# A bidirectional Gated DeltaNet layer on one core: chains emitted by a nominal clock, another way to the 4-block operand, low parts moved to VectorE, fewer row factors

## The chip, the cores and the metric

One core of a Trainium2 chip. TensorE (PE), VectorE (DVE), ScalarE (ACT), GpSimd (POOL) and SyncE (SP, which issues most DMA) each work through their own instruction stream in order. The metric is device microseconds of the whole program; the kernel before took 1396.1 us (median of three runs, 1393.63 to 1396.11).

## The reference

An encoder of two layers over 512 positions and 1024 channels, float32. Layer 0 mixes tokens by a bidirectional gated DeltaNet, layer 1 by a bidirectional gated linear attention (GLA); each is followed by a squared-ReLU MLP, and after each of the four sublayers comes a layer norm of `alpha * x + sublayer(x)`. The change lies in the DeltaNet layer, and in a helper for inverse square roots that all norms use. Of the DeltaNet, cut to what matters (8 heads, 128 channels each, both directions):

```python
qkv = silu(depthwise_conv(proj[..., :3072], conv_w))     # 5 taps
q, k = l2norm(q) * 128 ** -0.5, l2norm(k)
gc = cumsum(g)                                           # in a chunk
decay_mat = exp(where(causal, gc[:, None] - gc[None, :], -inf))
a_mat = where(strict, (k * beta) @ k.T * decay_mat, 0)
sol = triangular_solve(a_mat + I, [v * beta, k * beta * exp(gc)])
# scan over chunks:
v_new = u_c - w_c @ state
o = qd_c @ state + qk_c @ v_new
state = state * gl_c + kd_c.T @ v_new
# both directions added:
o = rmsnorm(o, norm_g) * silu(z);  out = o @ w_out
```

## The kernel before

The kernel takes chunks of 128 rows, so a head has 4 chunks (NT) in each of two directions, 8 units (U). Activations lie with channels on the partitions. Products that need more than one float pass are made in three (`mm3`, L109 to L111): the operands are split into a rounded high part and the rest (`split`, L90 on ScalarE and L91 on VectorE), and high x high, high x low and low x high are added. Weights come by DMA from SP in blocks of 512 KB, three buffers deep.

Per head there are these generators of class `GdnHead`:

- `project`: four projections of 24 matmuls each, tiles pjk, pjq, pjv, pjz; the convolution on ScalarE (L1077) and VectorE (L1081, four taps).
- `rows`: transposes of k and q (ktp), squares with row sums on ScalarE, then small row operations: the logarithms of the row factors, three bfloat16 parts of a row (rsp), their transposes (rtp), and the factors neg and kds.
- `solve`: kk = k k^T; the exponentials E of the decays for both directions (ep, L1208); at = E x kk without its diagonal (L1210); its float16 high part ath (a cast on ScalarE, L1212) and low part atl (a subtraction on GpSimd, L1213); a4, the 4 x 4 diagonal blocks of ath (L1216, all 8 units in one operation). From a4 come the inverses of the 4-blocks in three groups of products hp; then Dd, its transpose Xd (xp), and the inverse of the whole chunk by doubling over block sizes 4, 8, 16, 32 and 64 (products lv, L1265; L1274, L1284, L1285 on VectorE), one correction step with ath and atl (nw), and xf, the inverse as float32 (L1330).
- `recur`: four steps with three products each per direction (tiles m: m1 with the state, L1357; m2 with xf, L1365; m3 with k, L1377), with r on VectorE (L1359), vd and vn on ScalarE and the next state sn; then op, the head's output (L1390).
- `finish`: the RMS norm of op on ScalarE and VectorE (`rsqrt`, L167 to L173), the product fo, its transposes otp (L1413), the gate (L1415), and a split into oh and ol.

`out_pieces` (tile oa) multiplies heads 0 to 5 with w_out; `out_last` (tile ob) does heads 6 and 7 with the layer norm of each of the four row tiles behind it. The masks of the GLA layer (`sel_masks`, L504) are made on GpSimd, in the buffer of tag fo.

The order of the instructions is made in two stages. The program emits the generators in some order, and a scheduler then orders each engine's stream from that, by dependencies, free buffers and a priority that falls with the place in the emission. Before, `gdn` emits whole generators: in round i `recur` of head i-2, `solve` of head i-1, `project` and `rows` of head i, then `finish` of head i-2. The pairs of numbers that the generators yield are not read.

## Time and profile before

| what | value |
|---|---|
| median of three runs | 1396.1 us |
| profiled execution | 1403.4 us, span 1401.7 us |
| TensorE busy | 1361.3 us, 7917 matmul records |
| VectorE, ScalarE, GpSimd busy | 931.5, 693.9, 160.3 us |
| DeltaNet, its heads' stage | about 40 to 426 us of the span |
| of these 386 us | PE busy 377.1, DVE 296.8, ACT 246.6, POOL 37.4 |
| end of the DeltaNet, begin of the MLP | about 426 to 500 us, PE busy 63.1 of 74 |

A row of instructions names line, engine, operation, the tile written and the tiles read. A PE row's busy time runs to the modelled end of a pipelined matmul, so that consecutive ones overlap; start to start is the pace. A float32 product that isn't rounded stands as two records. The heads' stage has the only section in which many short chains over all engines run beside the large products.

### The profile page before, as it was taken

To read this page: it belongs to the slowest core of one execution; us is meant where nothing else is said; L and a number is where in the kernel's file an instruction comes from. 1 tells how busy PE (TensorE), PEld (TensorE's weight loads), DVE (VectorE), ACT (ScalarE), POOL (GpSimd) and SP (SyncE) were. 2 spreads that over 40 slices of the span, in tenths; PEclk is the share of its full clock that TensorE was granted. 3 is DMA by queue.
4 is the path that set the end of the run, shared out by engine and by line. 5 is a ranking of instruction groups with operands and counts; after the bars stand their busy time and mean duration, and the time that the engine had idled before them with its cause. 6 is when DMAs were issued, how large, how long until landed. Compare 5 with 4: busy or idle time off the path is not lost.

```text
span 1401.7 us, 20184 instructions
## 1 busy us (share of the span) xinstructions
PE 1361.3 (97%) x7917; PEld 1119.6 (80%) x7917; DVE 931.5 (66%) x1534; ACT 693.9 (50%) x1318; POOL 160.3 (11%) x228
## 2 busy tenths in 40 slices
PE   7999999999998989999999999999999999999997
PEld 6777777777776878888888888888879788888886
DVE  5787787778767355555655767977865555656655
ACT  3666657665733444444453255654433544545430
POOL 6000400000001301121000100000003111111000
PEclk9999999999999999999999999999999999999999
DMA  6312111111231955574513132212227776656121
GB/s 171 76 46 61 46 46 46 48 47 44 63 118 47 280 132 173 135 180 117 125 60 102 55 116 62 71 50 76 75 61 210 186 186 153 155 130 133 50 80 56
DMA packets 148055, 142.63 MB, mean 102 GB/s; under 512 B 9503, under 2 KB 124311, under 8 KB 147959
## 3 DMA queue, kind: packets, MB, share of 16 engines
q1 hardware_dynamic: 132224, 86.72, 21.7%
q0 software_dynamic: 15168, 54.54, 16.1%
q8 instruction: 62, 1.02, 0.3%
q14 instruction: 34, 0.28, 0.1%
q10 hardware_dynamic: 567, 0.08, 0.0%
HBM read 114.05 MB, written 2.10 MB: 83 GB/s over the span
## 4 chain that ended last, share of the span: by engine, by line
PE 80%; ACT 7%; DMA 4%; issue 4%; DVE 3%; POOL 1%; SPq 0%; DVEq 0%; POOLq 0%; ACTq 0%
PE pj L109 7%; PE pj L111 7%; PE pj L110 7%; PE pjv L109 3%; PE pjv L110 3%; PE pjv L111 3%; PE pX L110 2%; PE pX L109 2%; PE pX L111 2%; DMA w2r<-in_mlp_w 2%; PE pl L109 2%; PE pl L111 2%; PE pl L110 2%; PE scp L729 2%; PE op L1390 2%
## 5 line engine op out<-in xcount | busy, mean ns | idle before, releaser
L91 DVE TENSOR_TENSOR wl<-wst,wh 128x1024 fp32r<-128x1024 f32 x137 | 168.8, 1233 | 206.1 <-ACT wh L90 205.7
L90 ACT CAST wh<-wst 128x1024 fp32r<-128x1024 f32 x137 | 143.9, 1050 | 267.5 <-PE pj L110 168.7
L109 PE MATMUL pj<-xth,wh 128*128 128x512 f32 (+1 forms) x544 | 203.7, 375 | 8.0 <-ACT h L298 7.3
L111 PE MATMUL pj<-xth,wl 128*128 128x512 f32 (+1 forms) x544 | 202.8, 373 | 0.0
L110 PE MATMUL pj<-xtl,wh 128*128 128x512 f32 (+1 forms) x544 | 202.7, 373 | 0.0
L91 DVE TENSOR_TENSOR w2l<-w2r,w2h 128x1024 fp32r<-128x1024 f32 x84 | 102.6, 1222 | 80.6 <-ACT w2h L90 80.5
L109 PEld LDWEIGHTS pj<-xth,wh 128*128 128x128 f32 x544 | 103.1, 190 | 27.2 <-ACT h L298 8.5
L111 PEld LDWEIGHTS pj<-xth,wl 128*128 128x128 f32 x544 | 103.1, 190 | 18.2
L110 PEld LDWEIGHTS pj<-xtl,wh 128*128 128x128 f32 x544 | 103.2, 190 | 17.8
L90 ACT CAST w2h<-w2r 128x1024 fp32r<-128x1024 f32 x84 | 88.2, 1050 | 57.1 <-DMA w2r<-in_mlp_w 24.9
L329 POOL DMA_DIRECT2D w2r<-w2r x48 | 41.9, 912 | 274.0 <-DVE w2l L91 161.3
L90 ACT CAST ah<-h 128x1024 fp32r<-128x1024 f32 x40 | 42.2, 1054 | 41.6 <-PE pX L110 16.8
L110 PE MATMUL pX<-w2l,ah 128*128 128x512 f32 x144 | 56.1, 390 | 0.0
L109 PE MATMUL pX<-w2h,ah 128*128 128x512 f32 x144 | 56.1, 390 | 0.0
L111 PE MATMUL pX<-w2h,al 128*128 128x512 f32 x144 | 56.1, 390 | 0.0
L109 PE MATMUL pjv<-wh,xth 128*128 128x512 f32 x128 | 54.7, 428 | 0.0
L91 DVE TENSOR_TENSOR al<-h,ah 128x1024 fp32r<-128x1024 f32 x40 | 48.9, 1223 | 7.3 <-ACT ah L90 5.7
L1213 POOL TENSOR_TENSOR atl<-on,ath 128x512 f16<-128x512 f32 x16 | 20.9, 1308 | 282.5 <-PE m L1377 149.2
L168 ACT ACTIVATE rsy<-rsv 128x1 f32<-128x1 f32 (+1 forms) x28 | 5.7, 204 | 95.1 <-DVE rsv L167 95.0
L111 PE MATMUL pjv<-wh,xtl 128*128 128x512 f32 x128 | 50.2, 392 | 0.0
L110 PE MATMUL pjv<-wl,xth 128*128 128x512 f32 x128 | 49.9, 390 | 0.0
L312 POOL DMA_DIRECT2D w2r<-in_mlp_w x48 | 36.0, 768 | 115.5 <-DVE w2l L91 94.3
(436 smaller groups left out, 3483.1 us busy)
## 6 DMA issues: line engine op xcount, KB each, us to landing
wst<-in_mlp_w SPq DMA_DIRECT2D x80, 512.0 KB, 4.2
w2r<-in_mlp_w POOLq DMA_DIRECT2D x48, 512.0 KB, 4.6
w2r<-w2r POOLq DMA_DIRECT2D x48, 512.0 KB, 5.7
wst<-in_a_w_in SPq DMA_DIRECT2D x32, 512.0 KB, 4.0
wst<-in_b_w_in SPq DMA_DIRECT2D x32, 256.0 KB, 3.1
wst<-in_a_w_out SPq DMA_DIRECT2D x8, 512.0 KB, 3.8
wst<-in_b_w_in SPq DMA_DIRECT2D x8, 512.0 KB, 3.9
wst<-in_b_w_out SPq DMA_DIRECT2D x8, 512.0 KB, 3.6
```

The lines of the kernel that those rows point to most:

```text
L90: nc.scalar.copy(hi, src)
L91: nc.vector.tensor_tensor(lo, src, hi.bitcast(F32), ALU.subtract)
L109: mm(ps, ah, bh, start=start, stop=False, **kw)
L110: mm(ps, ah, bl, start=False, stop=False, **kw)
L111: mm(ps, al, bh, start=False, stop=stop, **kw)
L168: nc.scalar.activation(y, v, AF.Ln)
L312: nc.gpsimd.dma_start(t, w2[r:r + 2 * P, 512 * j:512 * j + 512].rearrange("(k p) n -> p k n", p=P))
L329: nc.gpsimd.dma_start(blocks[a + (q,)], blocks[b + (q,)], accum_op=ALU.add)
L729: T.matmul(ps[:, n, :], kh[:, sl], qh[:, sl], start=True, stop=True)
L1213: G.tensor_tensor(atl[:, us, :], at, ath[:, us, :], ALU.subtract)
L1390: T.matmul(op[:, n, :], l, r, start=i == 0, stop=i == len(mm) - 1)
```

## The change

1. **Emission.** `gdn` no longer emits whole generators. Six chains per head (project, rows, solve, recur, attend, finish), and the masks and the two halves of the output product, get a nominal start (40 units from head to head) and a factor. The one that is due first is advanced by one yield; its due time grows by the factor times the two numbers yielded. A yielded name waits until that step is done. The products op become a chain of their own, `attend`; `finish` of a head waits for a4 of the next, and `solve` of a head for `finish` two heads back.
2. **The 4-block operand.** kk is multiplied by a second mask (nd4: 4-blocks without the diagonal) into kk4, in the buffer fo; a4 is E x kk4, one operation per direction, written as float16. at and the cast to ath come behind it. The gate product p moves from the buffer on to fo.
3. **Low parts.** atl is subtracted on VectorE, emitted inside the solver's levels 8 and 16, and not on GpSimd.
4. **Row factors.** neg is no longer negated (signs go into qd, the states and sn), kds is one exponential without the product with beta, the factors -0.5 and the small constants go into existing operations, the RMS norm takes its epsilon as a tensor instead of multiplying by fq three times, and `rsqrt` has one operation less.

```diff
@@ rsqrt
-        nc.vector.tensor_scalar(v, x, scale, eps, ALU.mult, ALU.add)
-        nc.scalar.activation(y, v, AF.Ln)
+        if isinstance(eps, float):
+            nc.vector.tensor_scalar(v, x, -0.5 * scale, -0.5 * eps, ALU.mult, ALU.add)
+        else:
+            nc.vector.scalar_tensor_tensor(v, x, -0.5 * scale, eps, ALU.mult, ALU.subtract)
+        nc.scalar.activation(y, v, AF.Ln, scale=-2.0)
         nc.scalar.activation(y, y, AF.Exp, scale=-0.5)
         nc.vector.tensor_tensor(t, y, y, ALU.mult)
         nc.vector.tensor_tensor(t, t, v, ALU.mult)
-        nc.vector.tensor_scalar(t, t, -0.5, 1.5, ALU.mult, ALU.add)
-        nc.vector.tensor_tensor(out, y, t, ALU.mult)
+        nc.vector.scalar_tensor_tensor(out, t, 1.5, y, ALU.add, ALU.mult)
@@ gdn
-            if old:
-                run(old.recur(done))
-            if mid:
-                run(mid.solve(done))
-            if new:
-                run(new.project(done), new.rows(done))
...
-            if old:
-                run(old.finish(done))
+        T = 40
+        todo = []
+        for h, head in enumerate(heads):
+            todo.append([(h - 1) * T + 5, 1.8, head.project(done)])
+            todo.append([(h - 1) * T + 30, 1, head.rows(done)])
+            todo.append([h * T, 1, head.solve(done)])
+            todo.append([(h + 1) * T + 0, 1.5, head.recur(done)])
+            todo.append([(h + 1) * T + 30, 1.5, head.attend(done)])
+            todo.append([(h + 1) * T + 35, 1, head.finish(done)])
+        todo.append([2.5 * T, 1.0, masks()])
+        for hf in range(2):
+            todo.append([(A_H - 1 + hf) * T + 5, 1.8, output(hf)])
+        now = 0.0
+        while todo:
+            todo.sort(key=lambda x: x[0])
...
+            else:
+                todo[k][0] = t + scale * (step[0] + step[1])
@@ rows
-        V.tensor_scalar(lnr, ssp, 1e-6, None, ALU.add)
-        A.activation(lnr, lnr, AF.Ln)
-        V.tensor_scalar(lnr[:, 0, :], lnr[:, 0, :], -0.5, None, ALU.mult)
-        V.tensor_scalar(lnr[:, 1, :], lnr[:, 1, :], -0.5, -0.5 * math.log(P), ALU.mult, ALU.add)
+        A.activation(lnr, ssp, AF.Ln, bias=g.eps[:, 0:1])
...
-        A.activation(neg, rw, AF.Exp)
-        V.tensor_scalar(neg, neg, -1.0, None, ALU.mult)
-        V.tensor_tensor(kds, c0, g.tot[:, :, :, h], ALU.add)
-        A.activation(kds, kds, AF.Exp)
-        V.tensor_tensor(kds, kds, g.beta[:, :, :, h], ALU.mult)
+        A.activation(self.ew, rw, AF.Exp)
+        V.tensor_tensor(self.kds, cj, g.tot[:, :, :, h], ALU.add)
+        A.activation(self.kds, self.kds, AF.Exp)
@@ solve
+        kk4 = self.t2("fo", 1)
+        V.tensor_tensor(kk4, kk, g.nd4.unsqueeze(1).to_broadcast([P, NT, P]), ALU.mult)
+        kks = self.t2("on", 2)
+        V.tensor_tensor(kks, kk, g.nd.unsqueeze(1).to_broadcast([P, NT, P]), ALU.mult)
...
-            at = kks if d else self.t2("on", 2)
-            V.tensor_tensor(at, e, kks, ALU.mult)
-            us = slice(d * NT, (d + 1) * NT)
-            A.copy(ath[:, us, :], at)
-            G.tensor_tensor(atl[:, us, :], at, ath[:, us, :], ALU.subtract)
+            V.tensor_tensor(a4[:, dirs[d], :], e, kk4, ALU.mult)
             ex.append(e)
-        a4 = t8("a4", 1)
-        V.tensor_tensor(a4, ath, g.same4.unsqueeze(1).to_broadcast([P, U, P]), ALU.mult)
+        for d, e in enumerate(ex):
+            V.tensor_tensor(at[d], e, kks, ALU.mult)
+            A.copy(ath[:, dirs[d], :], at[d])
...
+            if s in (8, 16):
+                us = dirs[s // 16]
+                V.tensor_tensor(atl[:, us, :], at[s // 16], ath[:, us, :], ALU.subtract)
@@ finish
+        yield "op", self.h
+        if self.h < A_H - 1:
+            yield "a4", self.h + 1
...
-        V.tensor_tensor(ss, ss, self.fq, ALU.mult)
-        V.tensor_tensor(ss, ss, self.fq, ALU.mult)
-        c.rsqrt(rs_, ss, NT, 1.0 / P, RMS_EPS)
-        V.tensor_tensor(rs_, rs_, self.fq, ALU.mult)
+        c.rsqrt(rs_, ss, NT, 1.0 / P, self.heps)
```

Matmuls are the same in number (8843) in both programs. VectorE has 1478 instructions instead of 1536, GpSimd 218 instead of 233. SP's stream is the same.

Where instructions stand now. VectorE, head 4, from the kk products to the 4-block operand; first before (r and sn belong to the recurrence of head 3, sil to a convolution, on is at):

```order
L1359 SCALAR_TENSOR_TENSOR r<-m_3048,neg,vt 128x128
L1359 SCALAR_TENSOR_TENSOR r<-m_3052,neg,vt 128x128
L1195 TENSOR_TENSOR qd<-sil,qd 128x512
L1210 TENSOR_TENSOR on<-E,on 128x512
L1382 SCALAR_TENSOR_TENSOR sn<-sn,egl,m_3068 128x128
L1382 SCALAR_TENSOR_TENSOR sn<-sn,egl,m_3072 128x128
L1359 SCALAR_TENSOR_TENSOR r<-m_3076,neg,vt 128x128
L1359 SCALAR_TENSOR_TENSOR r<-m_3080,neg,vt 128x128
L1210 TENSOR_TENSOR on<-E,on 128x512
L1382 SCALAR_TENSOR_TENSOR sn<-sn,egl,m_3096 128x128
L1382 SCALAR_TENSOR_TENSOR sn<-sn,egl,m_3100 128x128
L1216 TENSOR_TENSOR a_3173<-ath,same_387 128x1024
```

and with the change:

```order
L1219 TENSOR_TENSOR on<-kk,nd 128x512
L1414 SCALAR_TENSOR_TENSOR sn<-sn,egl,m_3117 128x128
L1414 SCALAR_TENSOR_TENSOR sn<-sn,egl,m_3121 128x128
L1228 SCALAR_TENSOR_TENSOR qd<-sil,qd 128x512 x2
L1391 SCALAR_TENSOR_TENSOR r<-m_3138,neg,vt 128x128
L1391 SCALAR_TENSOR_TENSOR r<-m_3142,neg,vt 128x128
L1111 SCALAR_TENSOR_TENSOR sil<-pjq,cw,sil 128x511
L1242 TENSOR_TENSOR a_3156<-E,fo 128x512
L1111 SCALAR_TENSOR_TENSOR sil<-pjq,cw,sil 128x511
L1242 TENSOR_TENSOR a_3156<-E,fo 128x512
L1111 SCALAR_TENSOR_TENSOR sil<-pjq,cw,sil 128x510
L1245 TENSOR_TENSOR on<-E,on 128x512
```

The masked product fo<-kk (L1217) stands just ahead of the rows shown. The operand a comes from E in two halves, ahead of the products into on. VectorE again, head 4, from the inverse of the 4-blocks (Dd) into the solver's first level, before and with the change:

```order
L1231 TENSOR_TENSOR Dd<-dc,same_387 128x1024
L1081 SCALAR_TENSOR_TENSOR sil<-pjv,cw,sil 128x510
L91 TENSOR_TENSOR wl<-wst,wh 128x1024
L1274 TENSOR_TENSOR pz_174<-lv,off_397 128x2x64x4
L1081 SCALAR_TENSOR_TENSOR sil<-pjv,cw,sil 128x511
L1284 TENSOR_TENSOR Dd<-Dd,lv 128x2x64x4
```

```order
L1262 TENSOR_TENSOR Dd<-dc,same_389 128x1024
L1111 SCALAR_TENSOR_TENSOR sil<-pjv,cw,sil 128x510
L1317 TENSOR_TENSOR atl<-on,ath 128x512
L1303 TENSOR_TENSOR pz_174<-lv,off_400 128x2x64x4
L1317 TENSOR_TENSOR atl<-on,ath 128x512
L1313 TENSOR_TENSOR Dd<-Dd,lv 128x2x64x4
```

Both low parts stand around the first pz, earlier than the emission has them. TensorE at the stage's end, from the output op of head 7 (L1390 before, L1429 now) to its transposes otp; before, op and one L109 stand just ahead of the first row:

```order
L110 MATMUL ob<-wl,oh_423 128x512
L111 MATMUL ob<-wh,ol 128x512
L250 MATMUL ob<-z,ident 128x512
L109 MATMUL ob<-wh,oh_423 128x512
L110 MATMUL ob<-wl,oh_423 128x512
L111 MATMUL ob<-wh,ol 128x512
L250 MATMUL ob<-z,ident 128x512
L109 MATMUL ob<-wh,oh_423 128x512
L110 MATMUL ob<-wl,oh_423 128x512
L111 MATMUL ob<-wh,ol 128x512
L250 MATMUL ob<-z,ident 128x512
L1413 MATMUL otp<-ident,fo 128x128 x4
```

and with the change:

```order
L1429 MATMUL op<-sn,qd 128x128
L252 MATMUL ob<-z,ident 128x512
L109 MATMUL ob<-wh,oh_426 128x512
L110 MATMUL ob<-wl,oh_426 128x512
L111 MATMUL ob<-wh,ol 128x512
L252 MATMUL ob<-z,ident 128x512
L109 MATMUL ob<-wh,oh_426 128x512
L110 MATMUL ob<-wl,oh_426 128x512
L111 MATMUL ob<-wh,ol 128x512
L252 MATMUL ob<-z,ident 128x512
L1452 MATMUL otp<-ident,fo 128x128 x4
```

Nine products with weights and three with the identity stood between op and otp; now six and three do.

95 lines of the change are left out of this document (61 added, 34 removed).

## The prediction

> **What bounds the kernel now.** I read the first part of the page, then busy time by windows, then TensorE's waits in the DeltaNet stage. The page gives the profiled execution's span and the engines:
>
> ```profile
> span 1401.7 us, 20184 instructions
> PE 1361.3 (97%) x7917; PEld 1119.6 (80%) x7917; DVE 931.5 (66%) x1534; ACT 693.9 (50%) x1318; POOL 160.3 (11%) x228
> ```
>
> TensorE looks full, but its busy time counts the modelled tail of every matmul. The count of matmuls per window tells more. The windows below are the heads' stage of the DeltaNet, two steady heads in it, the next two, and 100 us of the MLP; PE's entry comes first, then weight loads, VectorE, ScalarE, GpSimd.
>
> ```profile
> 40.00:426.00 386.00, 377.14 (x3135) 296.32 (x3134) 296.83 (x642) 246.58 (x678) 37.40 (x55) 1.00 0.21 58
> 164.30:256.60 92.30, 89.46 (x762) 70.32 (x760) 73.44 (x159) 60.63 (x169) 4.66 (x4) 1.00 0.18 47
> 256.60:348.60 92.00, 89.17 (x762) 70.27 (x760) 73.40 (x159) 60.58 (x169) 4.67 (x4) 1.00 0.17 47
> 500.00:600.00 100.00, 100.00 (x438) 82.30 (x437) 61.24 (x61) 48.09 (x56) 13.72 (x17) 1.00 0.55 139
> ```
>
> In the MLP a 512-column matmul comes every 100/438 = 0.228 us and nothing else limits. A DeltaNet head takes 46.1 us for 381 matmul records. The pitch of short ones is in the chain of waits (the group's time over its count):
>
> ```profile
> 383.39 3.14 PE op L1390 x28
> 389.71 0.25 PE lv L1265 x8
> ```
>
> That is 0.112 us for 128-column float records and 0.031 us for the solver's. A head has 96 projection matmuls (21.9 us), 84 float records of 128 columns (9.4), 120 solver products (3.7) and 81 others, between 0.031 and 0.112 each (2.5 to 9.1): 37.5 to 44.1 us. So 2.0 to 8.6 us of each head is TensorE standing still inside its in-order stream, and VectorE, at 73.4 of 92.3 us, is busy but not the bound. TensorE's longest waits between 40 and 426 us (engine and line, waited for, us in total, times, longest):
>
> ```profile
> PE hp L1224 <- DVE a L1216: 2.2, 3, 0.9
> PE pjz L109 <- DVE sil L1081: 1.0, 3, 0.3
> PE m L1365 <- DVE r L1359: 0.9, 2, 0.5
> PE ktp L1127 <- ACT junk L1132: 0.9, 4, 0.2
> ```
>
> These are single links, and short. The number of matmuls does not change, so the change can only move such waits, in 8 heads, and shorten what TensorE waits for at the stage's end.
>
> **The change, part by part.** *The 4-block operand.* One of the three hp waits, head 4, in order of time:
>
> ```profile
> 240.95 0.65 ACT L1212 CAST ath<-on 128x512 f16<-128x512 f32 x1
> 241.68 1.16 POOL L1213 TENSOR_TENSOR atl<-on,ath 128x512 f16<-128x512 f32 x1 [1.88 <-ACT ath L1212]
> 241.95 1.44 DVE L1216 TENSOR_TENSOR a<-ath,same 128x1024 f16<-128x1024 f16 x1
> 243.44 0.35 PE L1224 MATMUL hp<-icc,a 128*128 128x4 f16 x8 [0.62 <-DVE a L1216]
> ```
>
> L1216 must follow the casts of both directions, and it slows down beside GpSimd's subtraction. All of its executions, L1210's and L1213's (ns minimum/median/maximum):
>
> ```profile
> L1216 DVE TENSOR_TENSOR a<-ath,same x8: 677/1342/1652, 72.1 to 378.6; 128x1024 f16<-128x1024 f16 x8
> L1210 DVE TENSOR_TENSOR on<-E,on x16: 679/705/1468, 68.1 to 376.4; 128x512 f32<-128x512 f32 x16
> L1213 POOL TENSOR_TENSOR atl<-on,ath x16: 1159/1166/2102, 69.7 to 378.7; 128x512 f16<-128x512 f32 x16
> L1202 DVE TENSOR_TENSOR on<-kk,nd x8: 679/688/692, 64.6 to 370.4; 128x512 f32<-128x512 f32 x8
> ```
>
> Now the operand is two products of 0.68 us (L1210's minimum, same size) straight from the exponentials, each releasing half of the hp group, and the casts come later. Between the last exponential and hp, a product, a cast of 0.65 and 0.7 to 1.65 us of L1216 become one product: about 1.5 us, against a longest wait of 0.9. What is late next are the exponentials:
>
> ```profile
> L1208 ACT ACTIVATE E<-ep,cj 128x128 f32<-128x128 f32 x64 | 19.5, 397 | 0.0
> ```
>
> Eight take 3.2 us, with a product and the steps between 4.4; the new order has hp's second half 5.7 us of TensorE work behind the first ep in heads 4 to 6, hp's first half 4.5 (four exponentials and a product, 2.6). Both fit, if ScalarE is free within a microsecond. I remove the 2.2 us; bounds 0 and -2.6 (three times 0.9).
>
> VectorE pays, per head, 0.69 for the second masked product of kk (L1202), two products of 0.68, and two low parts; before it ran L1216. The low part on VectorE is not in the trace. L1216 did twice the columns in 0.68, and L1210 the same columns in 0.68, so it costs 0.34 to 0.68; I take 0.68. That is 3.4 us added against 1.2 removed, and about nine row operations of 0.16 us (1.5) go. The net +0.7 us lies in a queue that is idle 9 us of each head, and counts nothing by itself; without that cover it would be 5.6 us over 8 heads.
>
> The page "SBUF — State Buffer" of the Trainium skill (section "SBUF: two separate sides") says that VectorE with two inputs in SBUF and GpSimd reading SBUF share an exclusive port pair: whoever comes second is held until the other has finished. The trace agrees: L1216 began 0.27 us into L1213's 1.16, and took 1.44 instead of 0.68. By that rule the whole excess of L1216 and L1210 ends with the move.
>
> *Low parts in front of the first solver level.* They stand in VectorE's order one before and one behind the first pz product (L1303 now, L1274 before). In heads 4 to 6 TensorE gives from the finished Dd to the product that needs pz: 8 transposes, 8 solver products, ten records of OP, about 0.45 + 0.25 + 1.12 = 1.8 us (the transposes at half of 0.112, an estimate). VectorE has a convolution tap, a low part and pz in that time, by these means:
>
> ```profile
> L1081 DVE SCALAR_TENSOR_TENSOR sil<-pjv,cw,sil 128x510 f32<-128x510 f32 (+1 forms) x32 | 23.8, 743 | 1.0 <-ACT sil L1077 0.9
> L1274 DVE TENSOR_TENSOR pz<-lv,off x24: 678/685/693, 78.6 to 392.5; 128x512 f16<-128x512 f32 x24
> ```
>
> 0.74 + 0.68 + 0.69 = 2.1 us, 0.3 too much, three times: +1.0. Bounds 0 and 16 x 0.68 = +10.9, if every low part delayed a level; behind pz wait only the level's own products and, on TensorE, all the filler that stands after them.
>
> *The nominal clock.* It respaces everything. Gone with the old alternation of odd and even heads may be the waits for r and junk above: of 1.8 us I take half, -0.9, bounds 0 and -1.8. New short distances arise: between the last nw group of heads 0, 2 and 6 and the m that reads its xf stand three 512-column products and one m, 0.9 us, where before 1.2 to 5.5 us of work stood. Such an xf, in head 7, and the product that follows it:
>
> ```profile
> 404.14 0.68 DVE L1330 SCALAR_TENSOR_TENSOR xf<-Xd,nw 128x512 f32<-128x512 f16 x1
> 404.31 0.40 PE L1329 MATMUL nw<-Xd,a 128*128 128x128 f16 x4
> 404.87 0.49 PE L1365 MATMUL m<-vt,xf 128*128 128x128 f32 x2
> ```
>
> An nw group lasts 0.40, xf 0.68, the step to m 0.05: 1.13 us against 0.9 + 0.2 of issue; 0.1 each if VectorE is free, 0.8 with one more operation ahead. Three times: +0.3 to +2.4; I take +0.6.
>
> *Fewer row factors.* Last head's normalisation, before:
>
> ```profile
> 422.80 0.16 DVE L1404 TENSOR_TENSOR oss<-oss,fq 128x4 f32<-128x4 f32 x1 [3.50 <-ACT junk L1402]
> 423.00 0.16 DVE L1405 TENSOR_TENSOR oss<-oss,fq 128x4 f32<-128x4 f32 x1
> 424.27 0.17 DVE L172 TENSOR_SCALAR rst<-rst 128x4 f32<-128x4 f32 x1
> 424.67 0.16 DVE L1407 TENSOR_TENSOR ors<-ors,fq 128x4 f32<-128x4 f32 x1
> 425.67 0.60 PE L1413 MATMUL otp<-ident,fo 128*128 128x128 f32 x4
> ```
>
> Four of eight small operations go, at 0.2 us from one to the next: 0.8 us. TensorE's order now has six instead of nine weight products ahead of the transposes; three of 0.228 are 0.7. I take -0.6, bounds 0 and -0.8. Every layer norm loses L172 as well, as at the end of the kernel, where nothing covers it:
>
> ```profile
> 1396.18 0.15 DVE L172 TENSOR_SCALAR rst<-rst 128x1 f32<-128x1 f32 x1
> 1396.37 0.16 DVE L173 TENSOR_TENSOR rstd<-rsy,rst 128x1 f32<-128x1 f32 x1
> 1396.57 1.41 DVE L199 SCALAR_TENSOR_TENSOR xt<-xt,rstd,ln 128x512 f32<-128x512 f32 x2
> ```
>
> 0.2 us there, 0.8 for the four norms that close the DeltaNet stage one after another, 0.4 for the other eight, mostly under matmuls: -1.4, bounds -0.2 and -3.2 (16 x 0.2).
>
> What the stage gains is not lost behind it: the MLP's first weights wait for the stage's end, since GpSimd issues them behind the last norm:
>
> ```profile
> 454.72 1.09 POOL L181 DMA_DIRECT2D ln<-in_ln_g  x2 [0.30 <-POOL xt L202]
> 457.58 9.12 DMA w2r<-in_mlp_w
> ```
>
> Sum: -2.2 + 1.0 - 0.9 + 0.6 - 0.6 - 1.4 = **-3.5 us**. The profiled execution took 1403.4 us (span 1401.7), 7.3 above the median of 1396.1; by it the changed one would take 1399.9, and the median 1392.6.
>
> **The rivals.** *VectorE pays out in full.* If VectorE's relief counts, because its in-order queue releases most links of the chain, L1216 and L1210 give 8 x (1.16 - 0.68) + 16 x (0.86 - 0.68) = 6.7 us more (means of the page of groups, below), to 1385.9. For it speaks that three of the four waits above end on VectorE; against it that VectorE is idle a fifth of the stage.
>
> ```profile
> L1216 DVE TENSOR_TENSOR a<-ath,same 128x1024 f16<-128x1024 f16 x8 | 9.3, 1160 | 0.4 <-ACT ath L1212 0.4
> L1210 DVE TENSOR_TENSOR on<-E,on 128x512 f32<-128x512 f32 x16 | 13.7, 856 | 0.1
> ```
>
> By the exclusive port of the Trainium skill's page "SBUF — State Buffer" (section "SBUF: two separate sides") this relief is certain on VectorE; whether the kernel's time follows, it doesn't say.
>
> *The clock only re-shuffles.* The instructions do stand elsewhere, but the hp waits are replaced by as many new ones: -1.4 - 0.6 of row work, +1.6 of new waits and nothing of the 3.1 removed: -0.4, 1395.7. For it: the waits are 9 us of 386 in all, and each is the length of one VectorE operation.
>
> *The low parts hold up the solver.* Each atl sits ahead of pz or of the Dd update on an in-order engine. If no distance hides one, +10.9 instead of +1.0: +6.4, 1402.5. It decides from 0.29 us per low part upward (4.5 us over 16), where the gain is gone. Against it: on GpSimd they ended long before use, and the order leaves VectorE waiting for lv there now.
>
> *The masks of the next layer.* They fill the buffer fo on GpSimd, which kk4 of head 3 now needs:
>
> ```profile
> 140.84 0.35 POOL L511 MEMSET fo<- 128x128 f32 x2 [31.23 <-PE otp L1413]
> 154.95 0.29 POOL L524 CAST mu<-fo 128x128 uint8<-128x128 f32 x1
> ```
>
> They take 14.4 us. Between head 1's otp and head 3's kk TensorE has 46 projection matmuls (10.5 us) and some 8 us of short ones, at the stage's real pace (46.1 us for about 40 of work) 21 us; of that head 1's transposes and the three operations behind them need 3 to 5. From 17 us of masks upward VectorE stops, and TensorE soon after; at 22, 5 us are lost: 1392.6 + 5 = 1397.6.
>
> **How the numbers follow.** My sum 0.43, VectorE in full 0.12, re-shuffle 0.25, low parts 0.15, masks 0.05. 0.2% (2.8 us, so 1393.3) is about what a measurement of this kernel can tell from no change. The sum's own range is 1389 to 1395; three quarters of it I put below 1393.3. Faster: 0.32 + 0.12 + 0.05 of the re-shuffle = 0.49. Same: 0.11 + 0.17 of the re-shuffle + 0.02 of the masks = 0.30. Slower: 0.15 + 0.03 of the re-shuffle + 0.03 of the masks = 0.21. Range: below, the relief with the favourable bounds of the norms, -13, 1383; above, the low parts' case, 1402.
>
> **What would show it.** Right: no wait of hp on the operand over 0.3 us, products into the operand and into at of 0.68 us, two heads in about 91.5 us, the gap from the last row operation to otp shorter by 0.8. Wrong: lv waiting for pz at the first level in heads 4 to 6 by more than 0.3, m for xf, or kk4 of head 3 standing on VectorE. If two heads take 90 us or less, respacing was worth more than I gave it; above 92.3, it cost.

## The result and the profile after

The changed kernel took 1382.8 us (median of five runs, 1380.9 to 1388.0) against 1393.9 (1393.4 to 1396.1) for the kernel before in the same comparison: 11.1 us less. The ratio of the two, 0.9904 with a 95% interval of 0.9875 to 0.9933, would be 9 to 17 us. The forecast was 1392.6, with a range of 1383 to 1402; the measured time lies just below it.

The page of the changed kernel, its span and engines; then busy time by windows (the heads' stage, two steady heads, the next two), and TensorE's waits between 40 and 416 us:

```profile
span 1381.1 us, 20067 instructions
PE 1354.1 (98%) x7917; PEld 1119.6 (81%) x7917; DVE 930.9 (67%) x1476; ACT 697.6 (51%) x1317; POOL 139.4 (10%) x213
```

```profile
40.00:416.00 376.00, 372.10 (x3127) 296.45 (x3126) 300.02 (x602) 248.42 (x675) 15.56 (x39) 1.00 0.22 60
161.10:250.40 89.30, 88.30 (x773) 70.58 (x769) 73.84 (x150) 61.18 (x169) 13.29 (x35) 1.00 0.17 43
250.40:339.40 89.00, 87.90 (x765) 70.81 (x762) 73.57 (x149) 61.23 (x169) 0.00 (x0) 1.00 0.17 48
```

```profile
PE lv L1296 <- ACT pz L1323: 0.9, 3, 0.3
PE lv L1296 <- ACT pz L1308: 0.9, 4, 0.3
PE ktp L1367 <- ACT junk L1164: 0.5, 2, 0.2
```

Two heads take 89.3 and 89.0 us instead of 92.3 and 92.0. The waits of hp for the operand, of m for r and of pjz for sil are gone from this list. VectorE's busy time is the same (930.9 against 931.5 us). The new and the moved products all take their 0.68 us, with nothing that stretches them (ns minimum/median/maximum):

```profile
L1242 DVE TENSOR_TENSOR a<-E,fo x16: 678/683/691, 65.9 to 367.2; 128x512 f16<-128x512 f32 x16
L1245 DVE TENSOR_TENSOR on<-E,on x16: 680/684/689, 66.5 to 367.8; 128x512 f32<-128x512 f32 x16
L1317 DVE TENSOR_TENSOR atl<-on,ath x16: 679/684/687, 72.2 to 371.4; 128x512 f16<-128x512 f32 x16
```

For the experiments one length is taken from each trace: the **stage**, from the first transpose of the gates (gtp) to the last otp. After, these two rows bound it, 414.70 - 26.24 = 388.5 us:

```profile
26.24 0.43 PE L968 MATMUL gtp<-ident,yr 32*128 32x32 f32 x4
...
414.70 0.60 PE L1452 MATMUL otp<-ident,fo 128*128 128x128 f32 x4
```

Before it was 425.67 - 27.8 = 397.9, so the stage gives 9.4 of the 11.1 us. From the last otp to the first MLP product it was 18.0 us, now 16.0. The last otp is a movable mark: of the 64 records of ob, 47 stood behind it before, 52 now, and all 64 in a_noclock, a_spread and a_round below. At the 0.228 us that a 512-column matmul takes in the MLP, five records are 1.1 us, moved from one length to the other; so the table below has both and their sum, which the change shortens by 11.4 us. The spans differ by more, 20.6 us, but the profiled execution before was 9.4 us over its median, and two waits of one kind in the MLP, behind the change, are the larger part of that; after, there is one, and it is short (us in total, times, longest):

```profile
PE pj L109 <- ACT h L298: 6.5, 2, 5.8
```

```profile
PE pj L109 <- ACT h L300: 1.8, 1, 1.8
```

From the first MLP product to the GLA layer's first pX it took 59.4 us in that one execution, and 49.1 to 55.0 in those of all other kernels here, most of which leave the MLP as it was. So the stage and the medians are compared, not the spans.

### The profile page after: what moved, and what is told of

Same layout as the page of the kernel before. It is cut to its first block, busy times and chain, and to the rows that moved or that the text cites. A ratio compares the mean times of both kernels' runs of the same rounds, so it can differ in the third digit from the quotient of the medians.

```text
span 1381.1 us, 20067 instructions
## 1 busy us (share of the span) xinstructions
PE 1354.1 (98%) x7917; PEld 1119.6 (81%) x7917; DVE 930.9 (67%) x1476; ACT 697.6 (51%) x1317; POOL 139.4 (10%) x213
## 3 DMA queue, kind: packets, MB, share of 16 engines
q0 software_dynamic: 15168, 54.54, 16.3%
## 4 chain that ended last, share of the span: by engine, by line
PE 86%; ACT 6%; issue 3%; DMA 2%; DVE 1%; POOL 1%; SPq 0%; DVEq 0%; POOLq 0%; ACTq 0%
PE pj L109 8%; PE pj L111 8%; PE pj L110 8%; PE pjv L109 3%; PE pjv L111 3%; PE pjv L110 3%; PE pX L110 2%; PE pX L109 2%; PE pX L111 2%; PE pl L109 2%; PE pl L110 2%; PE pl L111 2%; PE scp L731 2%; PE op L1429 2%; PE pZ L110 2%
## 5 line engine op out<-in xcount | busy, mean ns | idle before, releaser
L91 DVE TENSOR_TENSOR wl<-wst,wh 128x1024 fp32r<-128x1024 f32 x137 | 168.1, 1228 | 195.9 <-ACT wh L90 194.4
L90 ACT CAST wh<-wst 128x1024 fp32r<-128x1024 f32 x137 | 144.0, 1051 | 266.2 <-PE pj L110 163.3
L109 PE MATMUL pj<-xth,wh 128*128 128x512 f32 (+1 forms) x544 | 202.8, 373 | 1.8 <-ACT h L300 1.8
L91 DVE TENSOR_TENSOR w2l<-w2r,w2h 128x1024 fp32r<-128x1024 f32 x84 | 102.7, 1222 | 81.6 <-ACT w2h L90 81.6
L109 PEld LDWEIGHTS pj<-xth,wh 128*128 128x128 f32 x544 | 102.8, 189 | 20.0 <-ACT h L300 2.2
L90 ACT CAST w2h<-w2r 128x1024 fp32r<-128x1024 f32 x84 | 88.3, 1052 | 58.0 <-DMA w2r<-in_mlp_w 24.6
L90 ACT CAST ah<-h 128x1024 fp32r<-128x1024 f32 x40 | 42.3, 1057 | 40.3 <-PE pX L110 16.8
L109 PE MATMUL pX<-w2h,ah 128*128 128x512 f32 x144 | 56.1, 390 | 0.0
L109 PE MATMUL pjv<-wh,xth 128*128 128x512 f32 x128 | 54.7, 428 | 0.0
L91 DVE TENSOR_TENSOR al<-h,ah 128x1024 fp32r<-128x1024 f32 x40 | 48.9, 1223 | 7.3 <-ACT ah L90 5.7
L109 PE MATMUL pjk<-xth,wh 128*128 128x512 f32 (+1 forms) x112 | 42.5, 379 | 0.5 <-ACT wh L90 0.5
```

What stands on the lines that cost most here:

```text
L90: nc.scalar.copy(hi, src)
L91: nc.vector.tensor_tensor(lo, src, hi.bitcast(F32), ALU.subtract)
L109: mm(ps, ah, bh, start=start, stop=False, **kw)
```

## The experiments

Four theories stood at the start: the clocked emission gives the gain; the shorter chain from the exponentials to hp; VectorE's relief from GpSimd (the prediction's first rival); the row operations. Each part was taken out of the changed kernel (names with a_), then put alone into the kernel before (b_). The table has all runs; "ratio" is the time over that of the kernel before, with its 95% interval. The kernel before was measured again beside each group of runs (medians of 1395.2 to 1396.4), so a ratio tells more than the difference of two medians. The last three columns are of one execution each.

| kernel | median us | ratio | stage us | otp to MLP us | both us |
|---|---|---|---|---|---|
| before | 1393.9 | 1 | 397.9 | 18.0 | 415.9 |
| changed | 1382.8 | 0.9904 (0.9875 to 0.9933) | 388.5 | 16.0 | 404.5 |
| a_noclock | 1405.1 | 1.0077 (1.0057 to 1.0098) | 407.1 | 20.3 | 427.4 |
| a_oldblock | 1382.8 | 0.9913 (0.9896 to 0.9929) | 388.8 | 16.0 | 404.8 |
| a_poolatl | 1382.7 | 0.9915 (0.9897 to 0.9932) | 389.0 | 16.0 | 405.0 |
| a_oldrows | 1389.1 | 0.9956 (0.9935 to 0.9977) | 391.5 | 18.0 | 409.5 |
| b_clock | 1386.9 | 0.9930 (0.9905 to 0.9956) | 390.9 | 17.6 | 408.5 |
| b_block | 1405.1 | 1.0063 (1.0034 to 1.0093) | 407.6 | 18.0 | 425.6 |
| b_vecatl | 1392.7 | 0.9987 (0.9962 to 1.0012) | 394.3 | 18.0 | 412.3 |
| b_rows | 1390.4 | 0.9957 (0.9937 to 0.9978) | 396.3 | 16.3 | 412.6 |
| a_recurburst | 1388.2 | 0.9939 (0.9915 to 0.9963) | 391.2 | 16.2 | 407.4 |
| a_attend | 1385.9 | 0.9932 (0.9906 to 0.9958) | 389.8 | 16.7 | 406.5 |
| a_projburst | 1415.7 | 1.0139 (1.0111 to 1.0167) | 421.4 | 17.1 | 438.5 |
| a_projlate | 1396.2 | 1.0002 (0.9984 to 1.0020) | 400.3 | 16.7 | 417.0 |
| a_spread | 1390.2 | 0.9959 (0.9935 to 0.9983) | 392.4 | 20.3 | 412.7 |
| a_round | 1413.5 | 1.0120 (1.0092 to 1.0149) | 411.7 | 20.3 | 432.0 |
| a_p16 | 1384.9 | 0.9920 (0.9894 to 0.9947) | 388.7 | 16.7 | 405.4 |
| a_oldrsqrt | 1385.0 | 0.9919 (0.9892 to 0.9947) | 388.6 | 17.1 | 405.7 |
| b_spread | 1394.1 | 0.9988 (0.9974 to 1.0002) | 397.2 | 18.0 | 415.2 |
| b_clockrows | 1385.2 | 0.9921 (0.9890 to 0.9951) | 392.2 | 16.1 | 408.3 |

### One part undone in the changed kernel

**a_noclock**: `todo` and its loop go, whole generators are emitted as before.

```diff
-        todo = []
-        for h, head in enumerate(heads):
...
+        for i in range(A_H + 2):
...
+                run(old.recur(done), old.attend(done))
...
+                run(mid.solve(done))
...
+                run(new.project(done), new.rows(done))
```

> The changed kernel with its instructions written in the old order (the three neighbouring heads' generators one after another, TensorE's interleaving left to the scheduler as before; the next layer's masks ahead of head 1's finish); all arithmetic as changed. If the respacing by the nominal clock gave the gain of 1.5 us per head: two steady heads back from 89.2 to 91.5 us or more, the last otp at 423 us or later, the kernel +7 to +9 us. If the products or VectorE's relief gave it: two heads at most 90, at most +2 us. Rival 'everything together': about half, 90.3 us.

Measured: stage +18.6 us, two heads (the mean of heads 2 to 5, from kk to kk) 95.9 instead of 89.0, +22 us in all, more than twice what was expected, 4.3 of it behind the last otp, where 12 more records of ob stand. The clock is in the gain, and more than that: with the old order the other edits are 9 us slower than the kernel before.

**a_oldblock**:

```diff
-        kk4 = self.t2("fo", 1)
-        V.tensor_tensor(kk4, kk, g.nd4.unsqueeze(1).to_broadcast([P, NT, P]), ALU.mult)
...
-            V.tensor_tensor(a4[:, dirs[d], :], e, kk4, ALU.mult)
...
+        V.tensor_tensor(a4, ath, g.same4.unsqueeze(1).to_broadcast([P, U, P]), ALU.mult)
```

> The changed kernel with the 4-block operand made again from the cast operand by the mask same4 behind both casts, and no second masked product of kk; order by the clock and low parts on VectorE stay. If the shorter chain from the exponentials to hp gave the gain: hp waits again, 0.5 us or more in most heads, two heads 90.5 or more, +4 us or more. If the clock alone: hp has other work ahead and the two heads stay within 0.4 of 89.2, at most +1.5 us (VectorE even has one operation of 0.68 less per head).

Stage +0.3, time the same. Under the clock, and with the low parts on VectorE, the old way to the operand costs nothing, and hp does not stand in the list of waits either.

**a_poolatl**:

```diff
+            G.tensor_tensor(atl[:, dirs[d], :], at[d], ath[:, dirs[d], :], ALU.subtract)
...
-            if s in (8, 16):
-                us = dirs[s // 16]
-                V.tensor_tensor(atl[:, us, :], at[s // 16], ath[:, us, :], ALU.subtract)
```

> The changed kernel with the low parts back on GpSimd, directly behind each cast; the rest as changed. If 'VectorE pays out in full' is right (relief from slow operations beside GpSimd): some VectorE products of the solver's start go back to 0.8 to 1.4 us and the kernel gets 5 to 7 us longer, two heads 90.5 or more. If VectorE's time counts little: the products slow down as much, but two heads stay within 0.4 of 89.2 and the kernel within 1.5 us; VectorE even loses 2 x 0.68 us of work per head, so a gain of up to 1 us is possible.

Stage +0.5, time the same, and the products were not stretched, which neither theory had expected; GpSimd's operations were, somewhat:

```profile
L1242 DVE TENSOR_TENSOR a<-E,fo x16: 677/681/694, 65.9 to 367.8; 128x512 f16<-128x512 f32 x16
L1245 DVE TENSOR_TENSOR on<-E,on x16: 676/681/689, 66.5 to 368.4; 128x512 f32<-128x512 f32 x16
L1247 POOL TENSOR_TENSOR atl<-on,ath x16: 1155/1172/1559, 68.3 to 370.1; 128x512 f16<-128x512 f32 x16
```

They do still meet. One place, head 5 (start and duration in us):

```profile
281.72 0.68 DVE L1245 TENSOR_TENSOR on<-E,on 128x512 f32<-128x512 f32 x1
...
281.88 1.56 POOL L1247 TENSOR_TENSOR atl<-on,ath 128x512 f16<-128x512 f32 x1 [40.99 <-ACT ath L1246]
...
282.94 1.58 DVE L91 TENSOR_TENSOR wl<-wst,wh 128x1024 fp32r<-128x1024 f32 x1
```

The product began 0.16 us ahead and kept its 0.68 us; the low part, second, took 1.56 instead of 1.17; and the next large subtraction on VectorE, begun inside the low part, took 1.58 instead of its usual 1.23. Six of the 16 low parts come second like this (1.50 to 1.56 us). In the prediction's rows the low part was first, and L1216 took 1.44. So the order decides which of the two is first, and here it was the second that took longer.

**a_oldrows** (all of part 4 of the change but kds, which keeps its single exponential):

```diff
+        V.tensor_scalar(lnr, ssp, 1e-6, None, ALU.add)
+        A.activation(lnr, lnr, AF.Ln)
...
+        V.tensor_tensor(ss, ss, self.fq, ALU.mult)
+        V.tensor_tensor(ss, ss, self.fq, ALU.mult)
+        c.rsqrt(rs_, ss, NT, 1.0 / P, RMS_EPS)
+        V.tensor_tensor(rs_, rs_, self.fq, ALU.mult)
```

> The changed kernel with the row factors, the normalisation of the heads and the reciprocal root of every layer norm as before (only the factor beta stays folded in); order, 4-block operand and low parts as changed. If the small operations on VectorE release chain links: nine of 0.16 us per head come back, two heads 90 or more, +4 us or more in all. By the prediction's terms: the last head's normalisation +0.6 to +0.8, the norms +1.4, two heads within 0.3 of 89.2, so +2 us; the 2.9 us that were gained between the last otp and the first MLP product should come back wholly if the norms gave them.

+6.4 us: 3.0 in the stage, 2.0 between the last otp and the MLP, the rest in stretches where single executions scatter by as much. As in the kernel before, 47 records of ob stand behind the last otp here, five fewer than in the changed kernel, so some 1.1 us of the 3.0 belong to the second number.

### One part alone in the kernel before

**b_clock** has the new `todo` loop with the marks for it and all old operations. **b_block** has kk4 and the two products into a4, and with them what makes room: beta folded into the exponent, the gate product p in the buffer fo, the GLA masks emitted later in their round, and the casts and low parts behind the operand. **b_vecatl** moves the low parts to VectorE. **b_rows** has part 4. Their diffs are those of the change.

> The kernel before with the new order alone: the generators run by the nominal clock with the new due times and waits for marks; all operations as before (operand from the cast by same4, low parts on GpSimd, old row factors and norms). If the order by itself gives the gain (the old order with all other edits took 48.6 us per head and was 9 us slower than before): two heads 89.2 to 90, last otp at 417 to 419 us, the kernel -6 to -9 us. If order and operations only gain together: two heads above 91, at most -3 us.

> The kernel before with the 4-block operand made from the exponentials, a second masked product of kk, and the head's output product in buffer fo; beta folded into the exponent to make room; low parts still on GpSimd, order written as before. By the prediction's term: -2.2 us, hp no longer waits. By what the changed kernel in the old order showed (+9 us): slower by 3 us or more, with the solver's first levels waiting for work that now stands in front of them on VectorE and ScalarE.

> The kernel before with the low parts alone moved: subtracted on VectorE behind the solver's levels 8 and 16 instead of on GpSimd behind the casts. By 'VectorE pays out in full': L1216 falls from 1.16 us to 0.68 and L1210 from 0.86 to 0.68, -5 to -7 us. By the prediction's own terms: the hp wait shortens with L1216 (-1 to -2 us) against at most +1 for the low parts in front of pz: -1, within measurement. By 'low parts hold up the solver': +5 us or more.

> The kernel before with the row factors, the last head's normalisation and the reciprocal root of the norms as changed; the rest as before. Undone in the changed kernel it cost 6.4 us, with 0.7 of it inside the heads' stage, some 2 in front of the first kk and 3 behind the last otp. If those links stand alone: -4 to -6 us here too. If half of it came from the order chosen around them: -2 (the prediction's two terms together), two heads unchanged at 92.0 to 92.3.

Stages: -7.0, **+9.7**, -3.6, -1.6. Together that would be -2.5; the change has -9.4 (-4.6 against -11.4 with the stretch up to the MLP). The parts don't add, and what the operand is worth depends on the order around it.

b_block shows what came with an early result: hp no longer waits, but the recurrence does, and VectorE, behind the weights' high parts on ScalarE (L91 and L90 split the weights), waits 15.3 us where it was 9.8 before:

```profile
PE m L1366 <- DVE r L1360: 2.4, 3, 1.8
PE m L1378 <- ACT vn L1372: 1.8, 5, 0.5
PE rtp L1157 <- DVE rsp L1154: 1.5, 4, 0.5
...
DVE wl L91 <- ACT wh L90: 15.3, 13, 5.5
```

TensorE's stream tells where the work stands. From the first to the last recurrence product of heads 2 to 5 stand all 24 records of hp, against 8 or 16 before, and 13 to 15 projection matmuls against 17 to 24. That this order, and not the shared buffer fo, makes the 9.7 us is argued; no run here separates the two.

In b_vecatl the first rival's mechanism is there: without GpSimd beside them both operations are back at 0.68 us (maxima 0.77 and 0.80 instead of 1.65 and 1.47), as the rule of the exclusive port in the Trainium skill's page "SBUF — State Buffer" (section "SBUF: two separate sides") has it:

```profile
L1215 DVE TENSOR_TENSOR a<-ath,same x8: 683/684/773, 71.3 to 375.8; 128x1024 f16<-128x1024 f16 x8
L1210 DVE TENSOR_TENSOR on<-E,on x16: 679/684/801, 68.2 to 372.3; 128x512 f32<-128x512 f32 x16
```

hp hardly waits here either, with the old operand:

```profile
PE hp L1223 <- DVE a L1215: 0.2, 1, 0.2
```

The stretching was 6.3 us of VectorE's time; without it the stage is 3.6 us shorter, though the 16 low parts, 11.0 us, are now VectorE's own. The time moved by 1.8 (not told from nothing).

### What in the clock

First theory: the clock puts more projection matmuls (filler) under the recurrence. Each run changes the factor, the due time or both of one chain in `todo` (the names behind # are not in the code):

```diff
-            todo.append([(h + 1) * T + 0, 1.5, head.recur(done)])
+            todo.append([(h + 1) * T + 0, 0.05, head.recur(done)])      # a_recurburst
-            todo.append([(h + 1) * T + 30, 1.5, head.attend(done)])
+            todo.append([(h + 1) * T + 1, 0.05, head.attend(done)])     # a_attend
-            todo.append([(h - 1) * T + 5, 1.8, head.project(done)])
+            todo.append([(h - 1) * T + 5, 0.05, head.project(done)])    # a_projburst
+            todo.append([(h - 1) * T + 25, 0.05, head.project(done)])   # a_projlate
+            todo.append([(h - 1) * T + 5, 1.6, head.project(done)])     # a_p16
```

> The changed kernel with the recurrence of each head emitted nearly at once at its due time (its factor 1.5 becomes 0.05); every other chain by the clock as changed. In TensorE's order 10 to 16 projection matmuls then stand between the first recurrence product and the head's output, against 33 in the changed kernel, 17 to 24 before and 6 to 22 with the old order and new operations. If it is this filler under the recurrence that the clock brings: between the kernel before and the one in the old order, stage from the gates to the last otp 397 to 407 us against 388.5, the kernel +8 to +18. If the gain is the spacing of the projections or of the solver: within 2 us of the changed kernel.

> The changed kernel with the head's output products (attend) emitted directly behind the last recurrence step, no longer as a chain with a due time of its own. The filler under the recurrence stays at 33. If filler under the recurrence decides: stage 387 to 391 us, no change that can be measured. If it was the separate output chain that helped, because 28 long products then fill the solver's gaps: stage 393 us or more, +4 us or more.

> The changed kernel with each head's projections emitted nearly at once at their due time (factor 1.8 becomes 0.05); recurrence and solver by the clock. TensorE's order has 36 to 50 projection matmuls under the recurrence, but 20 to 30 fewer in the solver's levels and behind. If filler under the recurrence alone decides: stage within 3 us of 388.5. If filler must be spread over both chains: the waits move to the solver's products lv and to the start of rows (rtp), stage 394 to 402, +5 to +13 us.

> The same burst, but due 20 units later. In TensorE's order 51 to 54 projection matmuls stand ahead of the head's output, only 22 to 24 of them ahead of the last hp, and some 30 in the solver's levels. If filler anywhere in the recurrence is enough: within 3 us of 388.5. If spreading decides: 392 to 400, less than the early burst since the solver keeps more.

The counts in these expectations do not all hold in the traces: between the first recurrence product and the output of heads 2 to 5 the changed kernel has 43 to 46 projection matmuls, not 33, and a_recurburst 25 to 28, not 10 to 16 (16 to 22 of them up to the last recurrence product). The kernel before has 17 to 24, a_noclock 6 to 15. Head 4 of a_recurburst, all engines, then L109 alone (a third of the projection matmuls):

```profile
269.20:281.00 11.80, 11.80 (x74) 9.33 (x73) 8.73 (x28) 8.30 (x27) 0.00 (x0) 1.00 0.01 1
269.20:281.00 11.80, 2.23 (x6) 1.04 (x6) 1.00 0.01 1
```

So the first theory fell only for the filler above some 25 matmuls: without it the stage was 2.7 us longer, not 9 to 18. Less filler than that is not tested by itself. The separate output chain is worth 1.3 us of stage. But the projections in a burst cost 32.9 us, two and a half times the most that was expected, in waits of many kinds:

```profile
PE pjz L109 <- DVE sil L1111: 5.3, 3, 2.0
PE m L1409 <- ACT vn L1403: 4.1, 6, 1.1
PE lv L1296 <- ACT pz L1308: 2.3, 6, 1.0
```

The same burst 20 units later (a_projlate) cost only 11.8, and of these some 7.3 are the prediction's fourth rival: the GLA masks got the buffer fo late, kk4 of head 3 stood on VectorE, and r behind it:

```profile
182.65 0.21 POOL L513 MEMSET fo<- 128x128 f32 x1 [151.25 <-DVE ol L1456]
...
195.10 0.29 POOL L526 CAST mu<-fo 128x128 uint8<-128x128 f32 x1
...
DVE fo L1217 <- POOL mu L526: 8.1, 1, 8.1
...
PE m L1397 <- DVE r L1391: 7.3, 1, 7.3
```

Second theory: the even spread of the projections over recurrence and solver. **a_spread** gives the old rounds only that: `numbers` yields the sum of each step's two numbers, and `merge` advances the chain with the smallest total, factor times numbers. **a_round** merges recurrence and output, solver and projections as three chains, with the clock's factors 1.5, 1 and 1.8:

```diff
@@ a_spread
-        todo = []
...
+                parts += [old.recur(done), old.attend(done)]
...
+                parts.append(mid.solve(done))
+            both = [(0.6, numbers(*parts))] if parts else []
...
+                both.append((1.8, numbers(new.project(done))))
+            merge(*both)
...
+                run(new.rows(done))
@@ a_round
-        todo = []
...
+                parts.append((1.5, numbers(old.recur(done), old.attend(done))))
...
+                parts.append((1.0, numbers(mid.solve(done))))
...
+                parts.append((1.8, numbers(new.project(done))))
+            merge(*parts)
```

> The changed operations in the old order of rounds (recurrence, then solver, then row factors, then finish), with one thing from the clock: the projections of the next head are emitted evenly between the steps of recurrence and solver instead of behind them. TensorE's order has 23 projection matmuls ahead of the output and 66 by the solver's middle, against 6 to 22 and 14 to 38 in the old order. If an even spread of the projections is what the clock brings: stage from the gates to the last otp down from 407 us to 392 or less, kernel within 5 us of the changed one. If the other chains' places (finish, attend, row factors, overlap of rounds) bring it: 400 or more.

> The changed operations in the old rounds, and inside each round recurrence, solver and projections merged by the clock's factors (1.5, 1, 1.8); row factors and finish at the round's end as before. TensorE's order has 15 to 23 projection matmuls ahead of the first hp, 28 to 36 ahead of the output, 29 to 37 by the solver's middle. If merging by the clock inside a round is enough: stage 388 to 393 us. If the clock's gain needs row factors and finish merged too, or the projections spread evenly: 398 or more.

> The changed kernel with the projections emitted a little faster (factor 1.6 in place of 1.8), else the same; TensorE's order has 10 to 12 instead of 13 to 16 projection matmuls ahead of the first hp, 31 to 33 ahead of the output. If the spread has a broad optimum: stage 387 to 391 us, no measurable change. If the changed kernel sits on a narrow one: 393 or more, or a gain of 2 us or more.

The spread alone takes the stage from 407.1 to 392.4 us. Both runs have all of ob behind the last otp; with the stretch up to the MLP the spread gives 14.7 of the 22.9 us that the clock is worth there. The time is still 7.4 us over the changed kernel's, more than the 5 expected, so a third of the clock's worth lies elsewhere. The merge inside a round costs 4.6 us more than the old order (411.7): there the projections come behind, in the traces 25 to 48 from a head's first recurrence product to the middle of the next head's products lv (heads 1 to 4), against 66 to 69 in a_spread, 62 to 70 in the changed kernel and 14 to 40 in a_noclock. A factor of 1.6 gives 388.7, so the optimum is not narrow on that side. One rival stays: a_spread also has more filler under the recurrence than a_noclock (23 to 25 against 6 to 23) and fewer hp there (4 to 8 records against 16 to 24 in heads 1 to 5).

Two windows show it in TensorE's stream, each from the first recurrence product of a head to its last, in a_noclock and in the changed kernel: all engines, then L109 alone (a third of the projection matmuls), then tile hp (records in brackets):

```profile
284.60:296.40 11.80, 10.14 (x83) 8.21 (x82) 10.08 (x24) 8.39 (x23) 0.00 (x0) 1.00 0.01 3
284.60:296.40 11.80, 1.27 (x3) 0.56 (x3) 1.00 0.01 3
284.60:296.40 11.80, 1.03 (x24) 0.54 (x3) 1.00 0.01 3
```

```profile
267.60:286.00 18.40, 18.40 (x117) 14.60 (x116) 14.94 (x39) 12.38 (x38) 0.00 (x0) 1.00 0.11 29
267.60:286.00 18.40, 6.17 (x15) 2.65 (x14) 1.00 0.11 29
267.60:286.00 18.40, 0.85 (x17) 0.36 (x2) 1.00 0.11 29
```

In the old order the recurrence ran in 11.8 us with 3 products of L109 and the whole 4-block chain (24 hp) inside; VectorE was 85% busy, TensorE stood 1.7 us even by its padded count. With the clock it has 18.4 us, 15 of L109, 17 records of hp, 81% of VectorE, and TensorE does not stand by that count. Of the eight heads of a_noclock five have all 24 hp inside. A short recurrence alone does not make TensorE stand: in a_recurburst's window above it is as short, but no hp stands inside, VectorE is 74% busy, and TensorE has no stop by that count. VectorE's waits for ScalarE tell the same. In order, a_noclock (two rows), a_spread (two), the changed kernel (one; it has no row of rw):

```profile
DVE wl L91 <- ACT wh L90: 17.9, 12, 3.4
DVE rw L1150 <- ACT lnr L1143: 14.8, 5, 6.6
```

```profile
DVE wl L91 <- ACT wh L90: 4.5, 9, 0.9
DVE rw L1171 <- ACT lnr L1164: 2.0, 4, 0.5
```

```profile
DVE wl L91 <- ACT wh L90: 8.1, 11, 2.3
```

Both rows are operations of the projections' and the row factors' chains that stand early in VectorE's queue while ScalarE, in its own order, comes to their input late. a_round has 16.4 and 15.9 us of them. That these stops cause the recurrence's waits is argued from the order, not shown by a run of its own.

**b_spread** is the same spread in the kernel before:

> The kernel before, all its operations and its rounds, with only the projections of the next head emitted evenly between the steps of recurrence and solver. TensorE's order has 27 to 29 projection matmuls ahead of the head's output, against 17 to 24 before. If the even spread is what the clock brought on the old operations too (7.0 us of the stage): stage from the gates to the last otp 390 to 393 us against 397.9, the kernel -5 to -8. If the old operations, being spread already by the scheduler, gain from the clock in another way (finish, attend, row factors): 395 or more, at most -3.

Stage -0.7: no. The scheduler had spread the old operations nearly so by itself (in the traces, heads 1 to 4, 17 to 24 projection matmuls ahead of the output and 56 to 63 by the solver's middle; in b_spread 26 or 27, and 57 to 63). So what gives the clock's 7.0 us there stays open. The traces say where, not why. For this, add up, for each matmul record of the stage, the time from the one before it beyond the lower quartile for the same pair of shapes in all traces here, where that is over 60 ns. By this sum m2 behind r has 4.1 us before and 1.7 in b_clock, ktp 3.3 and 0.9, hp 3.8 and 2.6, nw behind Xd 1.5 and 0, while lv, m3 and op together rise by some 3. In all it falls by 4 us, so about half of the 7.0 escapes it.

**b_clockrows** (b_clock with part 4) and **a_oldrsqrt** (the changed kernel with the old `rsqrt`) size what is left:

> The kernel before with the clocked emission and the row edits, but with the old way to the operand (by same4 from the cast) and the low parts on GpSimd. If these two parts are the whole gain: the sum of what they gave alone (stage 397.9 - 7.0 - 1.6 to - 3.0, so 388 to 389.5 us; 1.7 us less between the last otp and the first MLP product), and a time within 1.5 us of the changed kernel's 1382.8. If the operand or the low parts are needed beside the clock: stage 391 or more, +3 us or more, with hp waits of 0.5 to 0.9 us.

> The changed kernel with the reciprocal root alone as before (one VectorE operation more in every layer norm and in each head's normalisation); all row factors as changed. With all row edits undone the kernel was 5 to 6 us longer: 3.0 in the stage, 2.0 between the last otp and the first MLP product, the rest at the end. If the norms carry it: +1 to +2 us between the last otp and the first MLP product, some 0.2 at the kernel's end, at most 1 in the stage, +2 to +3 in all. If the row factors carry it: within 1 us of the changed kernel everywhere.

Without operand and low parts on VectorE the stage is 392.2, 3.7 us over the changed kernel, and hp waits again:

```profile
PE hp L1251 <- DVE a L1242: 2.0, 5, 1.0
```

So these two parts have a share, though either can be missing alone: the hp wait goes with either of them (b_vecatl, b_block). In time it is +2.4 us, with intervals that overlap. The old `rsqrt` costs 1.1 us between the last otp and the MLP, 0.1 in the stage, +2.3 in all, again overlapping; the larger part of a_oldrows' 6.4 would then be the row factors'. No run beats the changed kernel measurably.

## Why the prediction was wrong

- **What bounds the kernel now.** "The change can only move such waits" is the step that failed. The listed waits of TensorE in the stage, the rows quoted and the shorter ones, add up to 6.7 us. By the sum over pairs of shapes described above, TensorE stood 49 us in the stage before (367 stops, half of them under 0.09 us), 41 after, 45 in b_clock, 60 in a_noclock. It is a modelled count: what the quartile itself holds of waiting is not in it. The prediction had the right bound beside it (2.0 to 8.6 us per head, 16 to 69 in all) and then worked with the list of waits, in which stops as short as these, under the modelled tail of the matmul before, do not appear. So the stops that the change could move were several times those that the forecast counted.
- **The nominal clock**, -0.9 (0 to -1.8): the term that was mis-sized most. It measured -7.0 of stage alone and 18.6 undone. The waits named, m for r and ktp for junk, are those that fell most in b_clock, but by 4.8 us together, not 0.9. The sentence "if two heads take 90 us or less, respacing was worth more than I gave it" came true, at 89.3 and 89.0. As a sign it was weak: b_vecatl, without the clock, has 89.6 from head 2 to head 6.
- **The 4-block operand**, -2.2: the wait went and the products took 0.68 us as forecast, but no run shows the price as the operand's own. Between b_clockrows (hp waits 2.0 us) and the changed kernel (none) lie 3.7 us, shared with the low parts; alone it is worth 0.3 undone (a_oldblock), and the low parts' move by itself takes the wait from 2.2 to 0.2 us (b_vecatl). That b_block is 9.7 us slower in the old order was not foreseen; its hp stand inside the recurrence.
- **Low parts in front of the first level**, +1.0: not there. No level waits for pz on VectorE; alone the move gave -3.6 of stage. The lower bound, 0, was the better value, and the relief of the products beside them was left to a rival.
- **New short distances from xf to m**, +0.6: no such wait is listed after, and by the sum over pairs m behind xf has 0.9 us, 1.4 before.
- **Row factors and norms**, -0.6 and -1.4: mis-sized. The tail of the last head is as forecast: from the first small operation to otp 2.87 us before, 2.2 now, where four operations stand instead of eight:

```profile
412.52 0.16 DVE L170 SCALAR_TENSOR_TENSOR rsv<-oss,fq 128x4 f32<-128x4 f32 x1 [0.64 <-ACT junk L1444]
413.19 0.16 DVE L173 TENSOR_TENSOR rst<-rsy 128x4 f32<-128x4 f32 x1 [0.51 <-ACT rsy L172]
413.39 0.16 DVE L174 TENSOR_TENSOR rst<-rst,rsv 128x4 f32<-128x4 f32 x1
413.59 0.16 DVE L175 SCALAR_TENSOR_TENSOR ors<-rst,rsy 128x4 f32<-128x4 f32 x1
413.78 0.69 DVE L1448 TENSOR_TENSOR fo<-op,ors 128x512 f32<-128x512 f32 x1
```

  But all of part 4 measured 6.0 us alone (3.1 to 8.8 by the ratio's interval) and 6.4 undone, against 2.0 forecast. For the norms behind the stage 0.8 was forecast; putting the old `rsqrt` back costs 1.1 there. The row operations in the heads were given nothing by themselves; undoing all of part 4 cost 3.0 of stage, of which 0.7 is the tail above and about 1.1 the five records of ob, so they are worth something like 1 us, and where the rest of the 6 lies stays open.
- **The rivals.** "VectorE pays out in full" had the mechanism (b_vecatl) but half its price, and under the clock it is gone (a_poolatl, +0.5); that its 1385.9 was the nearest of the forecasts, and that the range almost held, is luck. "The clock only re-shuffles" fell. "Low parts hold up the solver" fell. "The masks" did not happen in the changed kernel, but the mechanism is real and cost 7.3 us in a_projlate, where they began at 182.7 us. In the changed kernel they run from 166.7 to 180.2, and kk of head 3 begins at 184.1: a margin of 4 us.

## What to carry to other kernels

The list of waits is no ceiling for a change of order: take it from the pitch, records times their pace against the time that passes, before giving a respacing a price. Where long independent products run beside several short chains in in-order queues, spread them evenly over the chains by the program, not by what a scheduler thinks is idle: here that was worth 15 us of 407, and putting them in a block cost 33 in one place and, beside the masks' wait, 4.5 in another. Measure an edit under the order that it will live in: the new way to the operand went with +9.7 us in one and -0.3 in the other.

## What was not expected of the hardware

Low parts on GpSimd, directly behind the casts, slowed VectorE's products to 1.65 us before and not at all in a_poolatl (maximum 0.69), where GpSimd took up to 1.56 instead of 1.17 us: of a product and a low part that overlap, the one that began second was the longer one. Where L1216 and L1213 began within 0.05 us of each other, in heads 1 and 7 before, L1216 kept its 0.68 us, and L1213 took 1.73 and 1.67. And the profiled execution of the kernel before spent 4.4 us more from the first MLP product to the GLA layer than any of the 19 others: a single trace's span is a poor measure for 10 us.
